# First feed-forward's up stage: the plain weight piece loaded on GpSimd's queue, the activations' accumulating store issued behind the weights' accumulates, 0.82 modulation dots a piece, and the second group of activations fetched one per piece

## The chip, the cores and the metric

The kernel runs on 1 core of one Trainium2 chip. Five engines work beside each other, each through its own instructions in order: TensorE (PE in the profile, with its weight loads as PEld), VectorE (DVE), ScalarE (ACT), GpSimd (POOL) and SyncE (SP). An instruction that waits holds up everything behind it on its engine. SP and POOL also issue DMAs here, so a DMA that has to wait for a buffer holds up the DMAs behind it in the same way. The metric is the device time of the whole program in microseconds (us); lower is better.

## The reference, cut to what matters

One layer: a half-step feed-forward on 256 latent tokens and 256 context tokens, a token mixing of attention and Hyena, and a second half-step feed-forward on the latent tokens alone. Each is normed and modulated by vectors that come out of `SiLU(c) @ w_ada`. All is float32. The change touches the first feed-forward's up projection and the start of its down projection.

```python
def swiglu(h, w_up, w_down):
    gate, up = jnp.split(h @ w_up, 2, axis=-1)
    return (jax.nn.silu(gate) * up) @ w_down

def half_ffn(s, m, slot, g, w_up, w_down):
    h = modulate(rms_norm(s, g), chunk(m, 3 * slot), chunk(m, 3 * slot + 1))
    return s + 0.5 * chunk(m, 3 * slot + 2) * swiglu(h, w_up, w_down)
...
        mod = (s_lat @ w_ada[l] + b_ada[l])[:, None, :]
        mod_c = (s_ctx @ w_ada[l] + b_ada[l])[:, None, :]
...
        x = half_ffn(x, mod, 0, g_norm[l, 0], w_ffn1_up[l], w_ffn1_down[l])
        ctx = half_ffn(ctx, mod_c, 0, g_norm[l, 0], w_ffn1_up[l], w_ffn1_down[l])
```

with `D_MODEL = 2048` and `D_FF = 5632`.

## The kernel before

**Precision.** Each float32 operand is split into a rounded high part and the remainder (`hi`, `lo`), and a product is three matmuls: hi times hi, hi times lo, lo times hi (`mm3`, L247 to L249). Casts to `hi` are ACT's work. The remainder is a subtraction on DVE, except in two places of this stage, where ACT writes minus `hi` and an accumulating DMA adds the original to it. Only POOL issues such accumulating DMAs here.

**The up stage.** The 5632 hidden columns are 44 columns `j` of 128, gate and up together. Columns 0 to 2 run beside the start of the program; columns 3 to 43 run one after the other in `Ffn.up(j)`, each in four pieces `kq` of 512 KB of weights. From column 9 on (`QUADS`), pieces 1 to 3 are each done with seven products in place of eight, and their weights go through `quad_weights`: ACT casts `bhi` (L436) and `whi` (L465), DVE makes `blo` (L439), three sums (L442 to L444) and `wlo` (L471). Their raw tiles come in by SP and rotate over four buffers.

Piece 0 is the **plain** one. Its weights for column j+1 are made in column j, after piece 1 (`prepare(j + 1, 0)`): a load into the tile `plain`, of which there is one buffer, two casts by ACT (L425), two negations by ACT (L426) and two accumulating DMAs that POOL issues (L427, `u<-plain`). The next load into `plain` has to wait until both accumulates have read it. In the kernel before, that load is issued by SP (`weight_load`, L224), in the same queue as the raw tiles and the tiles of the dots.

**The dots.** The modulation vectors of later stages are dot products that DVE makes between the matmul pieces: one dot takes a 512 KB tile `adaw` (two buffers, loaded by SP at L144) and multiplies and sums it with the row of `SiLU(c)` (L151). After each piece `ada_hook` adds a rate to a counter (`ADA_RATES[0]`) and asks for a dot when the counter passes one. The stage needs 128 of them, and columns 4 to 43 call the hook 160 times.

**The activations.** At the end of column j `close` or the sums behind it make the activation, and `keep` writes it to DRAM (`actd[j]`) as `hi` and remainder: two stores by POOL (L534, L535) and an accumulating DMA onto the second (L536), which has to wait until that store has landed.

**The down stage.** Groups of four activations are read back (`fetch`, L551, two DMAs of 256 KB each), two groups ahead of their use. The first two groups (`ORDERS[0]` begins 9, 8) are fetched in column 43: the first group after piece 0, the second after piece 1. Both are POOL's.

**What sets the order.** The program is written in one order and a scheduler places the instructions on each engine by their dependences; `then(x, ...)` and `issue_after` pin an instruction behind another one. POOL's DMAs share eight semaphores in turn, so one waits for the landing of the one eight before it.

Of the kernel before, what the change touches and what calls it, by code (L numbers as in the profile page):

```python
# [12 lines left out]
F32R = mybir.dt.float32r  # L13
AF = mybir.ActivationFunctionType
ALU = mybir.AluOpType
# [3 lines left out]
P = 128  # L19
# [4 lines left out]
JT = FF // P  # L24
GRP = 4
# [6 lines left out]
WAVE = 3  # L32
ADA_UP = (5, 7, 6, 8)
ADA_DOWN = (2, 3, 4)
ADA_RATES = (0.79, 1.15, 1.42)
QUADS = {3: 5, 2: 7, 1: 9}
GT = JT // GRP
PASSES = ((0, 1, 2, 3), (4, 5, 6, 7))
ORDERS = ((9, 8, 10, 7, 6, 5, 4, 3, 2, 1, 0), tuple(range(GT)))
# [23 lines left out]
def hybrid_layer_kernel(ctx: ExitStack, tc: tile.TileContext, a):  # L63
    nc = tc.nc
# [56 lines left out]
    done = [0]  # L121
# [100 lines left out]
    def weight_load(src, shape, queue=None, pool=None):  # L222
        raw = T(wp, shape, "raw", bufs=4) if pool is None else T(pool, shape, "plain", bufs=1)
        load = (queue or nc.sync).dma_start(raw, src)  # L224
        loads.append(load)
        if done[0]:
            last_load[0] = load
        return raw

# [37 lines left out]
    def then(behind, do, *args, **kw):  # L267

        with tc.issue_after(behind.ins):
            return do(*args, **kw)  # L270
# [89 lines left out]
    class Ffn:  # L360
        def __init__(self, wup, wdown, cm, hook=None):
            self.wup, self.wdown, self.cm = wup, wdown, cm
            self.hook = hook or (lambda: None)
            self.h = [None] * KT
            self.mm = mm3
            self.held = {}
            self.sums, self.first, self.begun = {}, {}, None
            self.wupq = a["w_up1q"]

        def open(self, alt=False):  # L370
# [47 lines left out]
        def prepare(self, j, kq):  # L418

            pool = adap if kq == 0 and j > WAVE else None  # L420
            raw = weight_load(self.wupq[j - WAVE, kq], (P, 2, 4, P), pool=pool)
            if kq == 0:
                hi, lo = ([U((P, 4, P), F32R) for _ in range(2)] for _ in range(2))
                for q in range(2):
                    S.copy(hi[q], raw[:, q])  # L425
                    S.activation(lo[q], hi[q].bitcast(F32), AF.Copy, scale=-1.0)  # L426
                    nc.gpsimd.dma_start(lo[q], raw[:, q].bitcast(F32R), accum_op=ALU.add)  # L427
                return [(hi, lo)]
            if not self.quads(j, kq):
                return [weight(None, (P, 2, 4, P), raw=raw)]  # L430
            return raw
# [58 lines left out]
        def up(self, j):  # L490
            todo = [list(self.products(j, kq)) for kq in range(4)]
            left = [sum(t[0] == bank for piece in todo for t in piece) for bank in range(4)]
            total = list(left)
            banks = [(PA, PB)[j % 2]((P, 2, L)) if n else None for n in left]
            for kq in range(4):
                w = self.ahead if kq == 0 else self.quad_weights(j, kq) if self.quads(j, kq) else self.prepare(j, kq)
                for bank, part, n, q, block, x in todo[kq]:
                    ps = banks[bank] if part is None else banks[bank][:, part, :]
                    xx = self.h[x] if part is None else self.sums[x[0]][x[1]]
                    left[bank] -= 1  # L500
                    mm3(ps, [t[q][:, block] if kq == 0 else t[:, q, block] for t in w[n]], xx, left[bank] == total[bank] - 1, left[bank] == 0)
                if j == JT - 1 and kq < 2:
                    for n in range(GRP):
                        self.fetch(ORDERS[0], kq, n)
                if j < JT - 1 and kq == 1:
                    self.ahead = self.prepare(j + 1, 0)
                self.hook()
            for kq in QUADS:
                if QUADS[kq] == j + 1:
                    self.install(kq)  # L510
            if not total[2]:
                return self.close(j, banks)
            g, v, u = tmp((P, 2, L)), U((P, 2, L)), T(up, (P, L), "mt", bufs=3)
            S.copy(g[:, 0, :], banks[2][:, 0, :])
            V.tensor_add(u, g[:, 0, :], banks[2][:, 1, :])
            V.tensor_add(g[:, 1, :], u, banks[3][:, 0, :])
            V.tensor_add(v[:, 0, :], u, banks[3][:, 1, :])
            V.tensor_add(v[:, 1, :], g[:, 1, :], banks[3][:, 1, :])
            V.tensor_add(g, g, banks[0])
            V.tensor_add(v, v, banks[1])  # L520
            S.activation(g, g, AF.Silu)
            V.tensor_mul(v, v, g)
            self.keep(j, v)

        def keep(self, j, act):

            if j == JT - 1:
                for s_, t in enumerate(split(act, (P, 2, L))):
                    nc.gpsimd.dma_start(actd[j][:, s_], t)
                return  # L530
            hi, minus = U((P, 2, L), F32R), U((P, 2, L), F32R)
            S.copy(hi, act)
            S.activation(minus, hi.bitcast(F32), AF.Copy, scale=-1.0)
            nc.gpsimd.dma_start(actd[j][:, 0], hi)  # L534
            nc.gpsimd.dma_start(actd[j][:, 1], minus)  # L535
            nc.gpsimd.dma_start(actd[j][:, 1], act.bitcast(F32R), accum_op=ALU.add)  # L536

        def fetch(self, order, n, jj):

# [36 lines left out]
        def down(self, after):  # L576

            uses = [(p, g) for p in range(len(PASSES)) for g in ORDERS[p]]
            for n, (p, g) in enumerate(uses):
                if g == ORDERS[p][0]:  # L580
                    banks = {2 * dq + i2: (PA, PB)[k // 2]((P, 2, L)) for k, dq in enumerate(PASSES[p]) for i2 in range(2)}
                order = [q for _, q in uses]
                if g == ORDERS[p][5]:
                    for dq in PASSES[p]:
                        for i in range(2):
                            xs[i][dq] = U((P, 2, L))
                            nc.sync.dma_start(xs[i][dq], a["xT"][i, dq])
                at = n - len(uses) + APART
                if at == 0:
                    break  # L590
                for jj, dq in enumerate(PASSES[p]):
                    self.fetch(order, n + 2, jj)
                    self.hook(p)
                    self.step(g, dq, banks, g == ORDERS[p][0], g == ORDERS[p][-1] or at == -1)
            yield
            rest = [g for _, g in uses[-APART:]]
            for part in (1, 0):
                banks = {dq: (PA if part else PB)((P, 2, L)) for dq in PASSES[-1]}
                for g in rest:
                    for dq in PASSES[-1]:  # L600
                        self.step(g, dq, banks, g == rest[0], g == rest[-1], part, None if part else after)
                if part:
                    yield
# [1067 lines left out]
```

## Time and profile before

| | us |
|---|---|
| median of 3 runs | 2658.39 (2653.15 to 2658.84) |
| the profiled execution | 2656.8 |
| its span, first to last instruction | 2655.0 |
| PE busy | 2606.0 |
| DVE busy | 1892.0 |
| ACT busy | 1114.4 |
| POOL busy | 253.8 |

In the profile a row of the timeline or of a group has the line of the program, the engine, the operation and the tiles as out<-in; `SPq` and `POOLq` are the instructions that issue DMAs. A row of the waits says which instruction waited for which, the us in total, how often, and the longest. A row of the stages has the stretch, its length, the busy time of each engine with its instructions, the clock that TensorE was granted, and the DMA share and rate. The up stage of columns 3 to 43 runs from 154.8 to 1038.4 us.

### The profile page before, as it was taken

The numbers are of one execution on the slowest core, as the hardware profiler recorded it, in microseconds if no ns is written. First come the engines' busy times: TensorE is split into PE (matmuls) and PEld (weight loads), VectorE is DVE, ScalarE is ACT, GpSimd is POOL, SyncE is SP. The second block draws the span as 40 slices with busy tenths as digits, with TensorE's granted clock in tenths as the row PEclk, the third lists the DMA queues.
The fourth block names the chain that finished last, engine by engine and source line by source line (L and its number), as shares of the span: only waits on it lengthen the run. The fifth ranks groups of instructions, "written<-read, shape, count | busy, mean of one in ns | idle before, by whom it ended". The sixth has DMA issues, their size and how long they took to land.

```text
span 2655.0 us, 38017 instructions
## 1 busy us (share of the span) xinstructions
PE 2606.0 (98%) x14480; PEld 2238.3 (84%) x14480; DVE 1892.0 (71%) x3051; ACT 1114.4 (42%) x1543; POOL 253.8 (10%) x395
## 2 busy tenths in 40 slices
PE   8999999999999998999999999999999999999999
PEld 5678989989899897888888988888788888888887
DVE  6767788878788877777989796889665555554444
ACT  5344444444444443112211455456554444444333
POOL 1121111111111112320011000000000000000000
PEclk9999999999999998999999999999999999999999
DMA  9978778878788788996798555345555666566664
GB/s 371 360 221 254 222 214 266 242 225 242 222 243 239 232 248 285 395 385 202 258 326 288 177 175 191 122 131 162 173 183 190 191 190 189 188 188 207 203 200 157
DMA packets 193923, 607.67 MB, mean 229 GB/s; under 512 B 22315, under 2 KB 25356, under 8 KB 189388
## 3 DMA queue, kind: packets, MB, share of 16 engines
q1 hardware_dynamic: 140444, 504.40, 57.1%
q0 software_dynamic: 53104, 100.72, 15.6%
q8 instruction: 113, 1.85, 0.3%
q14 instruction: 70, 0.57, 0.1%
q10 hardware_dynamic: 192, 0.13, 0.0%
HBM read 545.10 MB, written 38.57 MB: 220 GB/s over the span
## 4 chain that ended last, share of the span: by engine, by line
PE 78%; issue 9%; DMA 5%; DVE 4%; ACT 2%; POOL 1%; SPq 0%; POOLq 0%; DVEq 0%; ACTq 0%
PE pa L1331 10%; PE pa L1332 10%; PE pa L1330 10%; PE pa L247 6%; PE pa L248 6%; PE pa L249 6%; PE pb L247 6%; PE pb L249 6%; PE pb L248 6%; PE pa L255 3%; DMA act<-u 2%; PE pa L257 2%; PE pa L1044 1%; PE pa L1045 1%; DMA adaw<-in_w_adaT_dram 1%
## 5 line engine op out<-in xcount | busy, mean ns | idle before, releaser
L240 DVE TENSOR_TENSOR wlo<-raw,whi 128x1024 fp32r<-128x1024 f32 x487 | 595.1, 1223 | 473.3 <-ACT whi L236 471.9
L236 ACT CAST whi<-raw 128x1024 fp32r<-128x1024 f32 x487 | 512.4, 1053 | 881.4 <-PE pa L1332 413.4
L1330 PE MATMUL pa<-whi,u 128*128 128x512 f32 x1060 | 413.9, 391 | 0.0
L1331 PE MATMUL pa<-wlo,u 128*128 128x512 f32 x1060 | 412.8, 390 | 0.2 <-DVE wlo L240 0.2
L1332 PE MATMUL pa<-whi,u 128*128 128x512 f32 x1060 | 412.9, 390 | 0.0
L247 PE MATMUL pa<-u,whi 128*128 128x256 f32 (+1 forms) x928 | 314.4, 340 | 7.5 <-ACT whi L465 3.8
L249 PE MATMUL pa<-u,wlo 128*128 128x256 f32 (+1 forms) x928 | 312.1, 337 | 4.2 <-DVE wlo L471 4.2
L248 PE MATMUL pa<-u,whi 128*128 128x256 f32 (+1 forms) x928 | 312.2, 337 | 3.6 <-DMA u<-act 3.1
L249 PE MATMUL pb<-u,wlo 128*128 128x256 f32 (+1 forms) x920 | 305.1, 332 | 7.4 <-DVE wlo L471 7.3
L247 PE MATMUL pb<-u,whi 128*128 128x256 f32 (+1 forms) x920 | 306.6, 334 | 4.6 <-ACT whi L465 4.5
L248 PE MATMUL pb<-u,whi 128*128 128x256 f32 (+1 forms) x920 | 304.5, 331 | 0.0
L1332 PEld LDWEIGHTS pa<-whi,u 128*128 128x128 f32 x1060 | 198.9, 188 | 41.5
L1331 PEld LDWEIGHTS pa<-wlo,u 128*128 128x128 f32 x1060 | 199.0, 188 | 41.4 <-DVE wlo L240 0.6
L1330 PEld LDWEIGHTS pa<-whi,u 128*128 128x128 f32 x1060 | 199.0, 188 | 40.7
L151 DVE CUSTOM_DVE_ANT_0 adas<-adaw,crow,cond 128x1024 bf16<-128x1024 f32 x160 | 204.8, 1280 | 32.2 <-DMA adaw<-in_w_adaT_dram 30.3
L151 DVE CUSTOM_DVE_ANT_0 adas<-adaw,crow,mod 128x1024 bf16<-128x1024 f32 x160 | 204.9, 1281 | 31.1 <-DMA adaw<-in_w_adaT_dram 29.0
L247 PEld LDWEIGHTS pa<-u,whi 128*128 128x128 f32 x928 | 178.2, 192 | 31.9 <-issue 4.9
L249 PEld LDWEIGHTS pa<-u,wlo 128*128 128x128 f32 x928 | 178.7, 193 | 23.2 <-DVE wlo L471 5.7
L249 PEld LDWEIGHTS pb<-u,wlo 128*128 128x128 f32 x920 | 176.4, 192 | 25.0 <-DVE wlo L471 9.1
L248 PEld LDWEIGHTS pa<-u,whi 128*128 128x128 f32 x928 | 178.6, 193 | 21.6 <-DMA u<-act 4.0
L247 PEld LDWEIGHTS pb<-u,whi 128*128 128x128 f32 x920 | 176.5, 192 | 23.0 <-ACT whi L465 5.6
L248 PEld LDWEIGHTS pb<-u,whi 128*128 128x128 f32 x920 | 176.6, 192 | 15.7 <-issue 0.4
(356 smaller groups left out, 4643.8 us busy)
## 6 DMA issues: line engine op xcount, KB each, us to landing
adaw<-in_w_adaT_dram SPq DMA_DIRECT2D x224, 512.0 KB, 5.8
raw<-in_w_dn_dram SPq DMA_DIRECT2D x184, 512.0 KB, 4.1
raw<-in_w_up_dram SPq DMA_DIRECT2D x176, 512.0 KB, 3.5
raw<-in_w_up1q_dram SPq DMA_DIRECT2D x124, 512.0 KB, 5.0
u<-act POOLq DMA_DIRECT2D x136, 256.0 KB, 11.3
act<-u POOLq DMA_DIRECT2D x131, 256.0 KB, 4.9
wrow<-in_w_ada_dram SPq DMA_DIRECT2D x32, 1024.0 KB, 9.9
plain<-in_w_up1q_dram SPq DMA_DIRECT2D x40, 512.0 KB, 3.6
```

The source lines that it names most:

```text
L151: V.tensor_tensor_reduce(out=sc, in0=t, in1=crow[i][:, b * (D // 2) : (b + 1) * (D // 2)], scale=1.0, scalar=mcol if b else bada[:, c * KT ...
L236: S.copy(hi, raw)
L240: last_lo[0] = V.tensor_sub(lo, raw, hi.bitcast(F32))
L247: PE.matmul(ps, w[0], xx[0], start=start, stop=False)
L248: PE.matmul(ps, w[0], xx[1], start=False, stop=False)
L249: return PE.matmul(ps, w[1], xx[0], start=False, stop=stop)
L255: PE.matmul(ps, w[0], x, start=start, stop=stop)
L257: PE.matmul(ps[:, 0, :], w[1], x[:, 0, :], start=False, stop=False)
L1044: PE.matmul(p_, hh, wlo[:, k2, :], start=False, stop=False)
L1330: PE.matmul(ps[t], hi, w[0], start=start, stop=False)
L1331: PE.matmul(ps[t], hi, w[1], start=False, stop=False)
L1332: last = PE.matmul(ps[t], lo, w[0], start=False, stop=stop)
```

## The change

There are four edits. The load of `plain` is issued by POOL (`nc.gpsimd`), and no longer counts as the last weight load behind which SP places the next dot's load. The accumulating DMA of `keep` is kept back in `self.unadded` and issued by `add_act` after piece 1 of the next column, behind the second of the plain accumulates (`self.added`); for the first three columns it is issued at once. The rate of the dots goes from 0.79 to 0.82. In column 43 the second group's activations are fetched one after each of the pieces 1 to 3, and the fourth at the first step of the down stage.

```diff
-ADA_RATES = (0.79, 1.15, 1.42)
+ADA_RATES = (0.82, 1.15, 1.42)
...
-        if done[0]:
+        if done[0] and queue is None:
             last_load[0] = load
...
-            raw = weight_load(self.wupq[j - WAVE, kq], (P, 2, 4, P), pool=pool)
+            raw = weight_load(self.wupq[j - WAVE, kq], (P, 2, 4, P), nc.gpsimd if pool else None, pool)
...
-                    nc.gpsimd.dma_start(lo[q], raw[:, q].bitcast(F32R), accum_op=ALU.add)
+                    self.added = nc.gpsimd.dma_start(lo[q], raw[:, q].bitcast(F32R), accum_op=ALU.add)
...
-                if j == JT - 1 and kq < 2:
-                    for n in range(GRP):
-                        self.fetch(ORDERS[0], kq, n)
-                if j < JT - 1 and kq == 1:
-                    self.ahead = self.prepare(j + 1, 0)
+                if j == JT - 1:
+                    for n in range(GRP) if kq == 0 else (kq - 1,):
+                        self.fetch(ORDERS[0], min(kq, 1), n)
+                if kq == 1:
+                    if j < JT - 1:
+                        self.ahead = self.prepare(j + 1, 0)
+                    self.add_act()
                 self.hook()
...
-            nc.gpsimd.dma_start(actd[j][:, 1], act.bitcast(F32R), accum_op=ALU.add)
+            self.unadded = j, act
+            if j < WAVE:
+                self.add_act()
+
+        def add_act(self):
+            if self.unadded:
+                j, act = self.unadded
+                self.unadded = None
+                then(self.added, nc.gpsimd.dma_start, actd[j][:, 1], act.bitcast(F32R), accum_op=ALU.add)
...
                 for jj, dq in enumerate(PASSES[p]):
+                    if (n, jj) == (0, 0):
+                        self.fetch(order, 1, GRP - 1)
                     self.fetch(order, n + 2, jj)
```

The first place is POOL's queue in the middle of the up stage, where column 9's activation (`act_37`) is stored and the plain piece for column 11 (`plain_3123`) is finished. Before:

```order
L534 DMA act_37_117<-u_3031 128x512
L535 DMA act_37_117<-u_3032 128x512
L427 DMA u_3127<-plain_3123 128x512
L536 DMA act_37_117<-u_3020 128x512
L427 DMA u_3128<-plain_3123 128x512
L534 DMA act_38_118<-u_3269 128x512
```

The same queue one column later in the changed kernel, from the plain load for column 12 (`plain_3362`) to the one for column 13. The accumulate onto the activation has the line of `then`, L270:

```order
L224 DMA plain_3362<-in_w_up1q_dram 128x1024
L536 DMA act_38_118<-u_3271 128x512
L537 DMA act_38_118<-u_3272 128x512
L427 DMA u_3366<-plain_3362 128x512
L427 DMA u_3367<-plain_3362 128x512
L270 DMA act_38_118<-u_3260 128x512
L224 DMA plain_3602<-in_w_up1q_dram 128x1024
```

The accumulate onto the activation no longer stands between the two accumulates of the plain piece but behind both, and the next plain load stands behind it.

The second place is SP's queue at the same time, around the first raw tile of column 12 after its plain piece (`raw_3375` before, `raw_3379` now). Before:

```order
L144 DMA adaw_3194<-in_w_adaT_dram 128x1024
L224 DMA raw_3375<-in_w_up1q_dram 128x1024
L224 DMA plain_3361<-in_w_up1q_dram 128x1024
L144 DMA adaw_3253<-in_w_adaT_dram 128x1024
L224 DMA raw_3434<-in_w_up1q_dram 128x1024
L144 DMA adaw_3373<-in_w_adaT_dram 128x1024
L144 DMA adaw_3430<-in_w_adaT_dram 128x1024
```

And in the changed kernel:

```order
L144 DMA adaw_3198<-in_w_adaT_dram 128x1024
L224 DMA raw_3379<-in_w_up1q_dram 128x1024
L144 DMA adaw_3305<-in_w_adaT_dram 128x1024
L224 DMA raw_3438<-in_w_up1q_dram 128x1024
L144 DMA adaw_3375<-in_w_adaT_dram 128x1024
L224 DMA raw_3547<-in_w_up1q_dram 128x1024
L144 DMA adaw_3434<-in_w_adaT_dram 128x1024
```

The plain load is gone from SP's queue, and dot loads and raw tiles follow each other there.

The third place is POOL's queue in column 43, from the store of column 42's activation (`act_70`) to the fetches of the down stage's first group (`act_64` to `act_67`) and second group (`act_60` to `act_63`). Before:

```order
L534 DMA act_70_150<-u_10870 128x512
L551 DMA u_10905<-act_64_144 128x512
L535 DMA act_70_150<-u_10871 128x512
L551 DMA u_10906<-act_64_144 128x512
L551 DMA u_10909<-act_65_145 128x512
L551 DMA u_10910<-act_65_145 128x512
L536 DMA act_70_150<-u_10859 128x512
L551 DMA u_10913<-act_66_146 128x512
L551 DMA u_10914<-act_66_146 128x512
L551 DMA u_10917<-act_67_147 128x512
L551 DMA u_10918<-act_67_147 128x512
L551 DMA u_10980<-act_60_140 128x512
```

And in the changed kernel, where the fetch has line 561:

```order
L537 DMA act_70_150<-u_10891 128x512
L561 DMA u_10924<-act_64_144 128x512
L561 DMA u_10925<-act_64_144 128x512
L561 DMA u_10928<-act_65_145 128x512
L561 DMA u_10929<-act_65_145 128x512
L561 DMA u_10932<-act_66_146 128x512
L561 DMA u_10933<-act_66_146 128x512
L561 DMA u_10936<-act_67_147 128x512
L561 DMA u_10937<-act_67_147 128x512
L561 DMA u_10997<-act_60_140 128x512
L561 DMA u_10998<-act_60_140 128x512
L270 DMA act_70_150<-u_10879 128x512
```

The eight fetches of the first group now follow each other, the accumulate onto column 42's activation stands behind them and behind the first fetch of the second group.

More of the change, by code (lines that the diff above doesn't have):

```diff
@@ L366, in __init__ @@
             self.held = {}
-            self.sums, self.first, self.begun = {}, {}, None
+            self.sums, self.first, self.begun, self.unadded = {}, {}, None, None
             self.wupq = a["w_up1q"]
```

## The prediction

> **What bounds the kernel now.** I start with the busy shares of the page.
>
> ```profile
> span 2655.0 us, 38017 instructions
> PE 2606.0 (98%) x14480; PEld 2238.3 (84%) x14480; DVE 1892.0 (71%) x3051; ACT 1114.4 (42%) x1543; POOL 253.8 (10%) x395
> ```
>
> TensorE is the bound, and the change leaves its matmuls alone. So it can only win back time in which TensorE waits or runs at a lowered clock. The next view is what TensorE waited for over the whole program.
>
> ```profile
> PE pb L249 <- DVE wlo L471: 7.3, 7, 1.8
> PE pb L247 <- ACT whi L465: 4.5, 4, 1.9
> PE pa L249 <- DVE wlo L471: 4.2, 5, 1.3
> PE pa L247 <- ACT whi L465: 3.8, 2, 1.9
> PE pa L248 <- DMA u<-act: 3.1, 2, 2.0
> PE pa L247 <- DMA u<-act: 1.7, 2, 0.9
> ```
>
> The first four rows are weights that came late in the up stage, 7.3 + 4.5 + 4.2 + 3.8 = 19.8 us. The last two are activations that came late at the start of the down stage, 4.8 us. To price the first kind I take the pace of the columns. These are the first matmuls of columns 9 and 43, and then eight columns and the start of the down stage as stages.
>
> ```profile
> 284.78 0.40 PE L247 MATMUL pb<-u,u 128*128 128x512 f32 x1
> ...
> 1017.82 0.40 PE L247 MATMUL pb<-u,u 128*128 128x512 f32 x1
> ```
>
> ```profile
> 325.94:352.15 26.21, 22.84 (x153) 21.28 (x151) 18.13 (x29) 9.67 (x15) 3.75 (x5) 0.93 0.76 212
> ...
> 434.47:455.05 20.58, 20.58 (x153) 19.62 (x151) 17.16 (x31) 9.89 (x15) 3.77 (x5) 1.00 0.91 264
> 579.26:606.98 27.72, 23.12 (x153) 21.35 (x152) 18.59 (x33) 9.68 (x15) 3.76 (x5) 0.94 0.70 202
> 710.22:736.91 26.69, 23.37 (x152) 21.38 (x151) 17.35 (x29) 9.65 (x15) 3.77 (x5) 0.94 0.75 210
> 757.50:779.09 21.59, 20.83 (x153) 19.67 (x151) 18.19 (x29) 9.68 (x15) 3.76 (x5) 1.00 0.84 236
> 861.53:888.13 26.60, 22.82 (x152) 21.25 (x151) 18.30 (x32) 9.66 (x15) 3.77 (x5) 0.94 0.74 220
> 991.03:1017.81 26.78, 22.82 (x152) 21.25 (x151) 18.35 (x31) 9.67 (x15) 3.77 (x5) 0.94 0.74 225
> ...
> 1042.60:1053.00 10.40, 7.73 (x17) 5.27 (x18) 5.64 (x12) 0.00 (x0) 1.58 (x3) 0.51 1.14 405
> ```
>
> A column without a wait takes 20.58 us, all of it TensorE's. From 284.78 to 1017.82 there are 34 columns with the same matmuls, 733.0 us in place of 34 x 20.58 = 699.7: **33.3 us too long**. The five columns of 26 to 28 us hold 134.0 - 5 x 20.58 = 31.1 us of it, the rest is 2.2. In those five the granted clock is 0.93 or 0.94 too, some 1.7 us a column beside the waits themselves.
>
> Now one of the five, from late matmul back to its cause. The rows are SP's queue, DVE, POOL's queue, ACT, and SP's waits between 200 and 1017 us.
>
> ```profile
> 317.24 0.33 SPq L224 DMA_DIRECT2D raw<-in_w_up1q_dram  x1
> 323.85 0.33 SPq L224 DMA_DIRECT2D plain<-in_w_up1q_dram  x1
> 324.27 0.38 SPq L144 DMA_DIRECT2D adaw<-in_w_adaT_dram  x1
> ```
>
> ```profile
> 329.65 1.28 DVE L151 CUSTOM_DVE_ANT_0 adas<-adaw,crow,mod 128x1024 bf16<-128x1024 f32 x1 [4.61 <-DMA adaw<-in_w_adaT_dram]
> ...
> 333.40 1.22 DVE L471 TENSOR_TENSOR wlo<-raw,whi 128x1024 fp32r<-128x1024 f32 x1
> ```
>
> ```profile
> 311.70 0.55 POOL L534 DMA_DIRECT2D act<-u  x1 [14.29 <-ACT u L532]
> ...
> 313.54 0.88 POOL L427 DMA_DIRECT2D u<-plain  x1 [0.62 <-ACT u L426]
> 317.86 0.88 POOL L536 DMA_DIRECT2D act<-u  x1 [3.44 <-DVE raw L442]
> 318.40 1.24 POOL L427 DMA_DIRECT2D u<-plain  x1
> ```
>
> ```profile
> 311.97 0.60 ACT L425 CAST u<-plain 128x512 fp32r<-128x512 f32 x1
> ...
> 314.38 0.63 ACT L426 ACTIVATE u<-u 128x512 fp32r<-128x512 f32 x1
> ```
>
> ```profile
> SPq L224 <- DMA u<-plain: 277.5, 45, 9.4
> ```
>
> DVE stood 4.61 us before a dot whose tile SP issued only at 324.27, and `wlo` is in DVE's queue behind the dot. SP issued it late because the plain load stood ahead of it and waited for the second plain accumulate, which POOL issued at 318.40. That one was ready when ACT's negation ended, 314.38 + 0.63 = 315.0, but stood behind the activation's accumulate, which waited for its own store. So one queue's order is passed on through four engines. SP waited in this way 277.5 us in all; mostly it costs nothing, because the next dot's tile is not yet needed. It costs where dots fall close together:
>
> ```profile
> 325.94:352.15 26.21, 4.95 (x4) 0.93 0.76 212
> 372.73:393.31 20.58, 3.84 (x3) 1.00 0.89 265
> 434.47:455.05 20.58, 4.82 (x4) 1.00 0.91 264
> ```
>
> These count the dots of a column, four in the long one and three in a common one; the third row shows four without a loss. 0.79 x 4 is 3.16 a column, so a fourth falls about every sixth column, and the long ones lie six to twelve columns apart.
>
> **The change part by part.** The sum is made against the profiled execution's 2656.8 us (span 2655.0), which is 1.6 below the median of the runs.
>
> *Plain load on POOL, activation's accumulate behind both plain ones.* SP loses 40 issues and with them the wait above; the dot's tile of 324.27 had a free buffer since the dot before the last had ended, and is then held only by raw tiles. On POOL one DMA a column is added and one moved. Durations from issue to landing:
>
> ```profile
> adaw<-in_w_adaT_dram SPq DMA_DIRECT2D x224, 512.0 KB, 5.8
> ...
> plain<-in_w_up1q_dram SPq DMA_DIRECT2D x40, 512.0 KB, 3.6
> u<-plain POOLq DMA_DIRECT2D x80, 256.0 KB, 5.9
> ...
> raw<-in_w_up_dram POOLq DMA_DIRECT2D x9, 512.0 KB, 8.3
> ```
>
> Follow the column that begins at 305.36. The second accumulate moves from 318.40 to 315.0 and lands 5.9 later, at 320.9; the activation's accumulate keeps 317.9, since its store sets it. The plain load waits behind both and for the landing: issue at about 321, against 323.85 on SP. No trace shows this load on POOL. Its nearest rows are the same tile on SP, 3.6, and a tile of that size on POOL, 8.3; I take 8.3, which was measured in the crowded start. It then lands at 329.3. ACT reaches the next plain cast 311.97 - 305.36 = 6.6 us into a column, so at 325.94 + 6.6 = 332.5. That leaves 3.2 us to spare, and 7.9 with the shorter landing: at both ends the load costs nothing. What is queued behind the waiting load on POOL are the next activation's stores, not due before 332. The accumulates themselves land at 321 for a column that begins at 325.94. So I take out all 33.3 us.
>
> The Trainium skill (SBUF — State Buffer, section "SBUF: two separate sides") speaks against this edit: it says that GpSimd is kept from writing its DMA descriptors while VectorE runs an fp32 operation of a certain mode, and advises the other queues. The profile shows POOL's accumulates issued all through a stage where DVE is busy for 17 of 20.58 us, in 0.88 to 1.24 us each; by the example in that page's next section, 620 ns grown to 3100, the load would come 2.5 us later, an estimate inside the 3.2. No row here separates the two.
>
> *0.82 dots.* Over 160 pieces the counter now gives ten columns of four dots, and the 128th dot is asked for in the first piece of column 43. Work on DVE grows by 0.12 dots or 0.16 us a column, in some 3 us of idle. A column of four dots that no plain load blocked lost nothing (434.47) or 1.01 us (757.50); I take the middle, 0.5, so ten cost **5 us**, with 0 and 10 as ends. The 2.2 us of small losses are part of this.
>
> *The fetches of column 43.* POOL's queue there, and the landing that the down stage waited for:
>
> ```profile
> 1027.70 1.60 POOL L551 DMA_DIRECT2D u<-act  x3
> 1032.12 0.89 POOL L536 DMA_DIRECT2D act<-u  x1 [2.81 <-DMA act<-u]
> 1032.68 4.04 POOL L551 DMA_DIRECT2D u<-act  x7
> ```
>
> The first group's last four DMAs stood behind the activation's accumulate at 1032.12, and the second group's followed at once and shared the engines with them. Now the eight follow each other, the last four about 1032.68 - (1027.70 + 1.60) = 3.4 us earlier, with two DMAs behind them in place of eight. The late landings cost 4.8 us of waits, and the granted clock of 0.51 over 10.40 us, with PE busy for 7.73 of them, 7.73 x 0.49 = 3.8. I take out **8.6 us**. What comes earlier in exchange is the second row of `SiLU(c)`, 1 MB, with dot tiles for the next stage, since the last dot no longer holds their memory; they are due when column 43's last piece is under way, and most of the first group has landed by then. The fourth activation of the second group now stands behind the stores of column 43's own, but is not used before the second group's turn, some 20 us into the stage.
>
> Sum: 2656.8 - 33.3 + 5 - 8.6 = 2619.9. **Forecast 2620 us**, 1.4% faster.
>
> **Rivals.** *The start of the down stage still waits*, because the earlier 1 MB load and dot tiles take the place of the second group: 2620 + 8.6 = 2629. For it: the DMA share there is 1.14 already. Against: the first group is issued 3 to 4 us earlier.
>
> *Denser dots stall where plain no longer does.* Raw tiles still stand ahead of dot tiles on SP and wait for DVE. If three of the ten columns lose what the five lose now, 31.1 / 5 = 6.2 each, it is 2620 + 18.6 = 2639.
>
> *Slower, by the dots' own landing.* If a dot's tile takes too long from a free buffer to landing, whatever stands ahead of it, every column of four dots stalls, and the change makes ten of them: 2656.8 - 33.3 + 62 - 8.6 = 2677. It decides once the landing of 5.8 us outlasts the time between the dot that frees a buffer and the one that wants it, two dots later, in these columns one to two pieces of 20.58 / 4 = 5.1 us. Against it stands 434.47, four dots and no loss. The Trainium skill (DMA: Bandwidth & Descriptors, section "Issuing engines are not separate DMA queues") would have it near this: issuing from several engines saves only the issue time. Here the issue time includes SP's waits of up to 9.4 us, so the trace bears that out only in small part.
>
> *Slower, by the plain load.* POOL serves it late: once it lands more than 3.2 us after 329.3, ACT stands in every column before L425, with TensorE's casts behind it. Two us in each of 39 columns give 2620 + 78 = 2698. Against it: 8.3 is the slower of the two rows, and still leaves 3.2.
>
> **How the numbers follow.** Forecast 0.67; down stage still waits 0.12; dots stall in three columns 0.10; dots' own landing 0.06, of which 0.02 with so few stalls that nothing changes; plain load 0.05. Faster by over 0.2% (about what a measurement of this kernel can tell from no change) are the first three, 0.89; within it 0.02; slower 0.09. The range goes from 2611 (no dot costs, 2614.9, and 3 to 4 us for the spread of the runs) to 2641 (the third case and 2 us), and leaves out 0.11.
>
> **What would show it.** Right: no wait for `u<-plain` among SP's, no DVE wait for `adaw` over 2 us, 34 columns at 20.6 to 21.2 us, plain loads landing before 7 us into the next column, no wait for `u<-act` in PE's and a clock of 1.00 around 1010 us. Wrong: ACT idle before L425, columns of four dots at 26 us, or a clock of 0.5 at the start of the down stage.

## The result, and the profile after

| | kernel before | changed kernel |
|---|---|---|
| median of the runs, us | 2658.61 (2653.15 to 2661.36, 4 runs) | 2630.74 (2625.92 to 2638.44, 4 runs) |
| ratio, 95% interval | | 0.990 (0.9871 to 0.9929) |
| profiled execution, us | 2656.8 | 2625.9 |

The change makes the kernel 1.0% faster; 1.4% was forecast. The profiled execution of the changed kernel is the fastest of its four. The page of that execution:

```profile
span 2624.1 us, 38011 instructions
...
PE 2592.5 (99%) x14480; PEld 2228.7 (85%) x14480; DVE 1891.7 (72%) x3051; ACT 1115.3 (43%) x1543; POOL 275.2 (10%) x435
```

The work is the same to the instruction on TensorE. What TensorE waited for from 154.7 to 1060 us, by line (us in total, times, longest):

```profile
PE pb L249 <- DVE wlo L471: 3.1, 7, 0.8
PE pa L249 <- DVE wlo L471: 2.8, 5, 0.8
PE pa L249 <- DMA u<-plain: 2.1, 1, 2.1
```

The waits of 1.8 and 1.9 us for `whi` and `wlo` are gone, and those for `u<-act`. One for the plain weights is left, in column 4; the kernel before has one of 1.5 us there. The program as stages of the changed kernel: columns 3 to 8, columns 9 to 42, one column of four dots, the longest column of all, 40 us around the start of the down stage, and all from column 43 on. A row has the length, the busy time of PE, PEld, DVE, ACT and POOL, then the granted clock, the DMA share and the rate in GB/s.

```profile
154.71:286.91 132.20, 130.11 (x685) 112.40 (x684) 93.72 (x162) 59.23 (x94) 30.42 (x44) 0.99 0.85 244
...
286.91:997.19 710.28, 704.29 (x5102) 668.23 (x5101) 589.45 (x1001) 332.55 (x476) 145.52 (x203) 1.00 0.86 246
...
557.18:579.49 22.31, 21.21 (x152) 19.78 (x151) 17.48 (x30) 9.67 (x15) 4.32 (x6) 1.00 0.74 222
641.21:663.56 22.35, 21.33 (x152) 19.76 (x151) 17.02 (x28) 9.68 (x15) 4.32 (x6) 1.00 0.72 202
...
1000.00:1040.00 40.00, 40.00 (x237) 35.70 (x236) 25.81 (x40) 12.82 (x16) 15.22 (x28) 1.00 1.00 336
...
997.19:2624.10 1626.91, 1615.38 (x7726) 1353.20 (x7724) 1100.21 (x1632) 651.49 (x847) 75.19 (x141) 1.00 0.66 214
```

The kernel before has these two for the first and the last stretch:

```profile
154.76:284.78 130.02, 128.57 (x685) 111.22 (x684) 93.34 (x161) 58.95 (x94) 27.20 (x38) 1.00 0.83 239
...
1017.82:2655.00 1637.18, 1621.37 (x7726) 1356.35 (x7724) 1105.24 (x1645) 651.21 (x847) 74.98 (x141) 1.00 0.66 214
```

So columns 9 to 42 give 733.0 - 710.3 = 22.7 us, the rest of the program 10.3, and columns 3 to 8 take back 2.2: 2655.0 - 22.7 - 10.3 + 2.2 = 2624.2, the span of 2624.1. Against 34 x 20.58 = 699.7 there are still 10.6 us in columns 9 to 42, where the forecast left 5. Where they are, in the column at 557.18 (SP's queue, DVE, PE; and DVE's wait for dot tiles between 200 and 1017 us, 46.0 in 19 in the kernel before):

```profile
550.22 0.33 SPq L144 DMA_DIRECT2D adaw<-in_w_adaT_dram  x1
```

```profile
557.90 1.28 DVE L151 CUSTOM_DVE_ANT_0 adas<-adaw,crow,cond 128x1024 bf16<-128x1024 f32 x1 [1.61 <-DMA adaw<-in_w_adaT_dram]
```

```profile
571.12 0.38 PE L249 MATMUL pa<-u,wlo 128*128 128x256 f32 x1 [0.76 <-DVE wlo L471]
```

```profile
DVE adas L151 <- DMA adaw<-in_w_adaT_dram: 13.5, 13, 1.8
```

The dot still came 1.61 us late, though nothing for `plain` stands in SP's queue now. All that follows on DVE came later with it; ACT waited 1.11 us for DVE's L524, cast the next `whi` later in turn, and `wlo`, which needs that cast, is late a piece later. Column by column, eight columns hold 10.1 of the 10.6 us, and each of them has, within 1.5 us of its start, a dot that waited 0.6 to 1.8 us for its tile. The number of dots in a column does not decide it, as the dots of the longest column and of one that lost nothing show:

```profile
641.21:663.56 22.35, 3.84 (x3) 1.00 0.72 202
432.36:452.94 20.58, 5.12 (x4) 1.00 0.86 243
```

The median of the runs is 4.8 us above this execution; a second profile, below, shows where a slower one loses it.

### The profile page after: what moved, and what is told of

The parts are those of the page before. It is cut to its first block, busy times and chain, and to the rows that moved or that the text cites. A ratio compares the mean times of both kernels' runs of the same rounds, so it can differ in the third digit from the quotient of the medians.

```text
span 2624.1 us, 38011 instructions
## 1 busy us (share of the span) xinstructions
PE 2592.5 (99%) x14480; PEld 2228.7 (85%) x14480; DVE 1891.7 (72%) x3051; ACT 1115.3 (43%) x1543; POOL 275.2 (10%) x435
## 4 chain that ended last, share of the span: by engine, by line
PE 84%; DVE 6%; DMA 5%; ACT 3%; issue 2%; POOL 0%; SPq 0%; DVEq 0%; ACTq 0%; POOLq 0%
PE pa L1343 10%; PE pa L1342 10%; PE pa L1344 10%; PE pb L247 7%; PE pb L249 7%; PE pb L248 7%; PE pa L247 7%; PE pa L249 7%; PE pa L248 7%; PE pa L255 3%; DMA adaw<-in_w_adaT_dram 2%; PE pa L257 2%; DVE wlo L471 1%; PE pa L1056 1%; PE pa L1057 1%
```

## The experiments

All times are medians, the ratios against the kernel before on the same chip (2658.31, 2660.46 and 2659.59 us in the three groups of four kernels each).

### Each part alone: the plain load, the accumulate, the fetch, the rate

The kernel before with the load of `plain` on POOL and nothing else:

```diff
-        if done[0]:
+        if done[0] and queue is None:
...
-            raw = weight_load(self.wupq[j - WAVE, kq], (P, 2, 4, P), pool=pool)
+            raw = weight_load(self.wupq[j - WAVE, kq], (P, 2, 4, P), nc.gpsimd if pool else None, pool)
```

> The kernel before with one edit: the plain load is issued by POOL. The activation's accumulate still stands between the two plain accumulates, the rate is 0.79, the fetches are as before. Theory SP (a waiting plain load holds up the dots' tiles behind it on SP): the five long columns go, the 34 columns from 9 to 42 take 702 to 708 us in place of 733, the start of the down stage keeps its waits, about 2658 - 27 = 2631 us. Rival POOL (the accumulate between the two plain ones is what makes the load late): the load is just as late, the long columns stay or turn into ACT's waits before the plain casts, 2650 us or more.

2646.63 us, ratio 0.9956 (0.9941 to 0.9971).

The kernel before with the activation's accumulate behind both plain ones, and nothing else:

```diff
-                if j < JT - 1 and kq == 1:
-                    self.ahead = self.prepare(j + 1, 0)
+                if kq == 1:
+                    if j < JT - 1:
+                        self.ahead = self.prepare(j + 1, 0)
+                    self.add_act()
...
-            nc.gpsimd.dma_start(actd[j][:, 1], act.bitcast(F32R), accum_op=ALU.add)
+            self.unadded = j, act
+            if j < WAVE:
+                self.add_act()
```

> The kernel before with one edit: the activation's accumulate is issued behind both plain accumulates. Plain stays on SP, rate 0.79, fetches as before. Theory SP: the second plain accumulate lands about 3.4 us earlier, so each long column keeps what is left of DVE's wait of 4.6 to 6.2 us, 31 us of losses fall to about 12, some 2640 us. Rival POOL: all five long columns go, about 2629 us. In column 43 the accumulate now stands behind the first group's fetches, so a part of the 8.6 us at the start of the down stage may go as well; I expect half of it, 4 us, in both.

2641.75 us, ratio 0.9937 (0.992 to 0.9953). Columns 9 to 42 of the first kernel, and of the second, which keeps the load on SP, with SP's wait there:

```profile
291.82:1006.72 714.90, 706.25 (x5103) 668.04 (x5102) 583.43 (x990) 334.28 (x476) 146.40 (x203) 1.00 0.87 241
```

```profile
285.17:1003.68 718.51, 707.75 (x5103) 671.32 (x5102) 583.79 (x989) 332.48 (x476) 127.65 (x170) 1.00 0.85 239
```

```profile
SPq L224 <- DMA u<-plain: 178.8, 41, 8.4
```

Either edit alone takes out about half of the 33.3 us: 15.2 are left with the load moved, 18.8 with the accumulate moved. The second shortens SP's wait from 277.5 to 178.8 us without touching SP's queue, as the chain of the prediction has it. The first misses its expectation by 16 us, and falls between the two theories. TensorE's waits for the plain weights in it, from 291.8 to 1006.7 us; its other waits there, 4.5 us, are for `wlo`:

```profile
PE pa L249 <- DMA u<-plain: 2.0, 2, 1.4
PE pb L249 <- DMA u<-plain: 1.5, 1, 1.5
```

The second plain accumulate still stands behind the activation's, so the plain weights themselves now come late at times, and ACT waited for the plain load before L425 eight times, 9.1 us in all, as the rival in the expectation has it. Columns 3 to 8 took 135.2 us (130.0 before), and the start of the down stage waits as it did, 5.3 us for `u<-act`.

The two edits that remain, each alone:

```diff
-                if j == JT - 1 and kq < 2:
-                    for n in range(GRP):
-                        self.fetch(ORDERS[0], kq, n)
+                if j == JT - 1:
+                    for n in range(GRP) if kq == 0 else (kq - 1,):
+                        self.fetch(ORDERS[0], min(kq, 1), n)
...
+                    if (n, jj) == (0, 0):
+                        self.fetch(order, 1, GRP - 1)
```

> The kernel before with one edit: the second group's activations are fetched one per piece. The accumulate onto column 42's activation still stands between the fetches of the first group. If the pile of sixteen fetches makes the first group late: no wait for u<-act, no lowered clock at the start of the down stage, 2658 - 8.6 = 2650 us. If the accumulate in the middle makes it late: about half of the 4.8 us of waits stays, and with it the lowered clock, 2655 us. The up stage's five long columns stay in both.

2658.77 us, ratio 1.0002 (0.9993 to 1.0012).

```diff
-ADA_RATES = (0.79, 1.15, 1.42)
+ADA_RATES = (0.82, 1.15, 1.42)
```

> The kernel before with one edit: 0.82 dots a piece. Theory SP: ten columns of four dots in place of six, behind a plain load that still waits on SP, so 8 to 10 long columns at about 6 us in place of five, less 2 us at the end of the stage: 2658 + 16 to 30 = 2674 to 2688 us. Rival (the long columns come from something that falls every sixth column and not from the fourth dot): 2657 to 2660 us.

2659.13 us, ratio 1.0003 (0.9993 to 1.0012). The start of the down stage with the fetch edit alone, and columns 9 to 42 with the rate alone:

```profile
1042.00:1056.00 14.00, 10.42 (x34) 7.40 (x35) 7.85 (x14) 2.11 (x3) 1.06 (x2) 0.76 1.12 404
```

```profile
286.50:1027.84 741.34, 716.01 (x5102) 677.62 (x5101) 589.96 (x1001) 332.11 (x476) 128.19 (x170) 0.99 0.83 237
```

The fetch edit alone leaves the wait (5.7 us for `u<-act`, 4.8 before) and the lowered clock, and neither of its two expectations came: the eight fetches of the second group were not what delayed the first. The rate alone costs 8.3 us in the columns (741.3 against 733.0), far less than expected: six of its twelve columns of four dots are long, by 4.7 to 7.7 us, where the kernel before has five of nine. It gains at the start of the down stage, as shown below, and no change of the whole can be measured. The four parts sum to -11.7 - 16.6 + 0.5 + 0.8 = -27.0; the changed kernel has -27.9.

### The changed kernel again

> The changed kernel as it is, beside the kernel before in many more rounds, and as the kernel that the next three are read against. From its own 2630.7 us: 2627 to 2635, 0.99 of the kernel before. A second profile tells whether its 10.6 us over 34 x 20.58 in columns 9 to 42 and the late start of columns 3 to 8 (2.2 us over before) come back, or were of that one execution.

2631.56 us, ratio 0.9902 (0.9887 to 0.9917), as before. Its profiled execution was the slowest of the five, 2638.75 us. Columns 3 to 8, 9 to 42, and the rest:

```profile
155.66:292.71 137.05, 131.25 (x686) 113.27 (x684) 93.79 (x162) 59.47 (x94) 30.43 (x44) 0.98 0.83 235
...
292.71:1005.17 712.46, 705.51 (x5102) 668.49 (x5101) 589.07 (x1000) 333.03 (x476) 145.44 (x203) 1.00 0.86 245
...
1005.17:2637.00 1631.83, 1620.38 (x7726) 1357.25 (x7724) 1100.39 (x1633) 652.85 (x847) 75.11 (x141) 1.00 0.67 214
```

Beside the first profile of the changed kernel, 4.9 us more are in columns 3 to 8, 2.2 in columns 9 to 42, and 4.9 in the rest. The rest has a lowered clock far behind the change: 0.90 over the stretch from 1500 to 1550 us, where the first profile had 1.00 and the kernel before 0.97. The same wait of TensorE stands ahead of it in all three, 2.5 us for a `wlo`, and the 20 us behind that wait differ (the kernel before, the first and the second profile of the changed one):

```profile
1538.00:1558.00 20.00, 19.95 (x90) 16.63 (x91) 16.77 (x32) 10.03 (x19) 0.00 (x0) 0.92 0.59 171
```

```profile
1508.00:1528.00 20.00, 19.93 (x96) 16.67 (x97) 18.09 (x36) 11.38 (x21) 0.00 (x0) 1.00 0.62 186
```

```profile
1516.00:1536.00 20.00, 19.95 (x74) 16.67 (x75) 13.32 (x27) 8.27 (x16) 0.00 (x0) 0.74 0.52 158
```

So 0 to 5 us are won or lost there from one execution to the next, whatever the change does; on this point the first profile was lucky. Columns 3 to 8 are near the change, and are taken up below.

### What is left in columns 9 to 42: the rate, and the number of buffers

The changed kernel with the old rate:

```diff
-ADA_RATES = (0.82, 1.15, 1.42)
+ADA_RATES = (0.79, 1.15, 1.42)
```

> The changed kernel with the old rate 0.79, so six to seven columns of four dots in place of ten. Buffer theory (each column of four dots still costs about 1 us, because a tile can only be asked for when the dot two before it has ended): columns 9 to 42 lose some 4 us less than in the changed kernel, 6 to 7 in place of 10.6, and about 3 us come back as dots left over at the end of the stage, so the time is within 3 us of the changed kernel's. Rival, that the rate carries part of the gain by itself: 5 us or more slower than the changed kernel. Rival, that denser dots cost what the long columns of before did: 10 us or more faster.

2633.27 us, ratio 0.9901 (0.9887 to 0.9914). Columns 9 to 42:

```profile
290.03:995.75 705.72, 703.67 (x5103) 668.14 (x5101) 583.20 (x989) 333.59 (x476) 145.50 (x203) 1.00 0.85 243
```

6.0 us over 699.7, as the buffer theory has it. The rest took 1632.3, with 2.7 us of waits for `u<-act`, and the whole comes out the same: 0.82 moves lost time from the start of the down stage into the columns.

Then three buffers for the dots' tiles, paid for with two buffers `u`, and as a control the two `u` fewer alone:

```diff
-        return T(up, shape, "u", dt, 58)
+        return T(up, shape, "u", dt, 56)
...
-    adap, adaw_bufs = adap_cm.__enter__(), 2
+    adap, adaw_bufs = adap_cm.__enter__(), 3
```

> The changed kernel with three buffers for the dots' tiles in place of two; the 56 in place of 58 buffers u pay for the memory. Buffer theory: the rest of 10.6 us over 34 x 20.58 in columns 9 to 42 falls under 4, DVE's waits for adaw from 13.5 us in 13 to under 4, the longest under 1, and the kernel is 6 to 8 us faster than the changed one. Rival, that DVE is simply full in a column of four dots (17 us of work and its order): the excess stays at 9 to 11 us though the waits for adaw are gone, same time. Rival, that two u fewer make ACT or POOL wait: slower, with waits for u that were not there.

2633.45 us, ratio 0.9902 (0.9887 to 0.9917).

> The changed kernel with 56 in place of 58 buffers u and nothing else, to tell what the three-buffer run paid for its memory. Theory that the two buffers u were what it lost: a column 9 of about 25 us with DVE waiting for act<-u at L395, columns 9 to 42 at some 15 us over 34 x 20.58, 3 to 6 us slower than the changed kernel. Rival, that the third buffer does nothing for the time and the u are enough: same as the changed kernel.

2643.10 us, ratio 0.9938 (0.9925 to 0.995). Columns 9 to 42 and column 9 alone, then DVE's waits for DMAs from 284 to 1017 us; first with three buffers and 56 `u`, then with two buffers and 56 `u`:

```profile
293.19:1001.85 708.66, 703.98 (x5103) 669.18 (x5102) 590.86 (x1005) 336.59 (x477) 145.56 (x203) 1.00 0.87 246
293.19:318.64 25.45, 22.39 (x152) 21.03 (x151) 18.70 (x32) 9.95 (x15) 4.31 (x6) 0.93 0.78 221
```

```profile
DVE u L395 <- DMA act<-u: 2.3, 1, 2.3
```

```profile
292.81:1012.61 719.80, 709.31 (x5102) 671.28 (x5101) 591.04 (x1004) 334.13 (x477) 145.26 (x203) 1.00 0.85 243
292.81:319.46 26.65, 23.73 (x153) 22.27 (x151) 18.77 (x32) 9.92 (x15) 4.30 (x6) 0.87 0.78 224
```

```profile
DVE adas L151 <- DMA adaw<-in_w_adaT_dram: 12.9, 11, 2.6
DVE u L395 <- DMA act<-u: 2.8, 1, 2.8
```

With the third buffer DVE has no wait for `adaw` left. Without column 9 the excess is 708.7 - 25.5 - 33 x 20.58 = 4.1 us; with two buffers and the same `u` it is 719.8 - 26.7 - 679.1 = 14.0. So the third buffer is worth 9.7 us where the `u` are equal (2643.1 against 2633.5), and two `u` fewer cost 11.5 (2643.1 against 2631.6): 6.1 of it in column 9, where DVE waits for a buffer that an accumulate onto an activation still reads; where the rest lies the profiles don't settle. The two cancel, and the expected 6 to 8 us did not come. The rival, that DVE is simply full, falls: the same work on DVE took the shorter time.

### The fetches, in the changed kernel

The changed kernel with the second group fetched at once after piece 1:

```diff
-                if j == JT - 1:
-                    for n in range(GRP) if kq == 0 else (kq - 1,):
-                        self.fetch(ORDERS[0], min(kq, 1), n)
+                if j == JT - 1 and kq < 2:
+                    for n in range(GRP):
+                        self.fetch(ORDERS[0], kq, n)
...
-                    if (n, jj) == (0, 0):
-                        self.fetch(order, 1, GRP - 1)
```

> The changed kernel with the second group's eight fetches after piece 1 at once, as before; the other three edits stay. Theory that the accumulate in the middle of the first group's fetches was what made the down stage wait: same time within 1 us, since the accumulate now stands behind both groups, at most 2 to 3 us of waits for u<-act and no lowered clock at the start of the down stage. Rival, that the eight fetches at once take the first group's bandwidth: waits of 4 us and a clock of 0.5 as before, 5 to 8 us slower.

2629.83 us, ratio 0.9891 (0.9878 to 0.9905). Column 43 and the first 40 us of the down stage:

```profile
999.14:1060.00 60.86, 60.86 (x330) 52.98 (x329) 43.84 (x70) 17.89 (x21) 20.05 (x37) 1.00 1.00 339
```

TensorE is busy throughout, at a clock of 1.00, without the fetch edit. Together with the run of the fetch edit alone this settles that fetching one per piece adds nothing measurable. The accumulate that no longer stands among the first group's fetches is not the whole of the rest, though. The 60 us from column 43 on with the accumulate moved alone, the rate alone, and the changed kernel at the old rate:

```profile
1003.68:1063.68 60.00, 57.11 (x310) 48.97 (x309) 47.16 (x76) 16.79 (x20) 18.95 (x35) 1.00 1.01 347
```

```profile
1027.84:1087.84 60.00, 57.44 (x300) 49.28 (x299) 38.58 (x61) 16.60 (x20) 22.91 (x43) 0.94 1.03 344
```

```profile
995.75:1055.75 60.00, 57.29 (x304) 48.97 (x303) 45.99 (x75) 16.59 (x20) 18.69 (x35) 0.97 1.03 352
```

In each some 2.6 to 2.9 us of waits for `u<-act` are left. Counted over the first 300 matmuls from column 43 on, the kernel before took 63.97 us and the changed one 54.61; the accumulate alone took 58.38, the rate alone 60.60, the changed kernel at the old rate 59.75. So the accumulate's place brings 5.6 of the 9.4 us by itself, the rate 3.4, and only both together bring all. How the rate does it, no run tells; with it fewer dots are left over behind the columns.

### Column 4

A column 4 without waits takes 21.76 us. It took 23.55 in the kernel before, and 25.73 and 30.57 in the two profiles of the changed one. SP's queue, POOL's queue and PE in the slower of the two (the third fence is the row of the DMA view between 160 and 190 us, its last number the median us from issue to landing, as in the rows of that kind further on):

```profile
168.88 5.77 SPq L224 DMA_DIRECT2D raw<-in_w_up1q_dram  x2
175.52 0.33 SPq L144 DMA_DIRECT2D adaw<-in_w_adaT_dram  x1
```

```profile
175.40 0.88 POOL L270 DMA_DIRECT2D act<-u  x1 [6.98 <-DMA act<-u]
175.95 2.14 POOL L427 DMA_DIRECT2D u<-plain  x2
...
183.86 0.80 PE L249 MATMUL pa<-u,u 128*128 128x512 f32 x1 [5.80 <-DMA u<-plain]
```

```profile
u<-plain POOLq DMA_DIRECT2D x2, 256.0 KB, 8.9
```

In the first profile that median is 7.8 us. In the kernel before, SP's waits from 155 to 185 us and the same landing:

```profile
SPq L224 <- DMA u<-plain: 37.1, 2, 21.0
```

```profile
u<-plain POOLq DMA_DIRECT2D x2, 256.0 KB, 5.3
```

The accumulates of the first three columns still stand ahead of the plain ones and wait for their stores, in both kernels. But before, SP stood still for 21.0 us at the plain load for column 5, and nothing of its own was under way when the plain accumulates were issued; now it loads raw and dot tiles there. The other profiles agree: column 4 takes 25.7 to 30.6 us in all seven profiles with the plain load on POOL and these accumulates in place, and 22.4 to 23.6 in the four with the load on SP. Two runs take this apart. First, the first columns' accumulates held back like the others:

```diff
-            self.unadded = j, act
-            if j < WAVE:
-                self.add_act()
+            self.unadded.append((j, act))
...
-            if self.unadded:
-                j, act = self.unadded
-                self.unadded = None
+            for j, act in self.unadded:
...
+            self.unadded = []
```

> The changed kernel with the accumulates onto the activations of columns 0 to 2 held back too and issued behind both plain accumulates of column 4, as for every later column. Theory that they stand ahead of these on POOL's queue and wait for their stores: the wait for u<-plain in column 4 (5.8 us in the last profile of the changed kernel, 2.1 in the first) goes, with the lowered clock at 182 us; columns 3 to 8 take 128 us in place of 132 to 137; 5 to 7 us faster than the changed kernel, 2624 to 2627. Rival, that the plain weights of column 4 come late because of other transfers, whatever stands ahead: column 4 stays at 25 us or more, same time.

2627.21 us, ratio 0.9882 (0.9869 to 0.9896). Then one load back on SP:

```diff
-            raw = weight_load(self.wupq[j - WAVE, kq], (P, 2, 4, P), nc.gpsimd if pool else None, pool)
+            raw = weight_load(self.wupq[j - WAVE, kq], (P, 2, 4, P), nc.gpsimd if pool and j != WAVE + 2 else None, pool)
```

> The changed kernel with one load put back: the plain piece of column 5 is loaded by SP again, all others by POOL. In the kernel before, SP stood at this load from 159.7 to 180.8 us and issued nothing. Theory that this wait kept raw tiles and dots' tiles off the DMA engines while the plain accumulates of column 4 were under way: they land within 5 us of their issue again (7.9 in the changed kernel), column 4 takes 23 to 24 us in place of 25.7 to 30.6, and the time is 2 to 6 us below the changed kernel's. Rival, that the accumulates are slow because of the stores and accumulates on POOL's own queue around them: no change.

2624.77 us, ratio 0.987 (0.9856 to 0.9883). The plain accumulates on POOL and column 4 as a stage in the first of these runs, then SP's wait (155 to 185 us), the landing and column 4 in the second:

```profile
163.88 0.88 POOL L427 DMA_DIRECT2D u<-plain  x1 [0.65 <-ACT u L426]
165.05 0.87 POOL L427 DMA_DIRECT2D u<-plain  x1 [0.29 <-ACT u L426]
```

```profile
176.90:198.66 21.76, 21.76 (x97) 18.02 (x96) 15.24 (x25) 10.20 (x17) 4.86 (x7) 1.00 0.96 273
```

```profile
SPq L224 <- DMA u<-plain: 20.7, 1, 20.7
```

```profile
u<-plain POOLq DMA_DIRECT2D x2, 256.0 KB, 5.5
```

```profile
177.93:201.30 23.37, 22.06 (x98) 17.95 (x96) 14.71 (x25) 10.08 (x17) 4.42 (x7) 1.00 0.96 252
```

Both theories hold. Issued 12 us earlier, the plain accumulates may take as long as they like; issued late as ever, but with SP standing still, they land in 5.5 us and not in 8.9. One load put back on the queue that the change cleared makes the kernel faster than the changed one, with intervals of the ratio that just don't meet (0.9883 and 0.9887). The interval of the changed kernel's first four runs is wider and does meet it, but eight of its nine executions took longer than the longest of these four. The other run shows its gain in the profile, but its interval overlaps that of the changed kernel.

### Both together

The accumulates held back, with three buffers for the dots' tiles and 56 `u` (the edits of above):

> The changed kernel with both: the first columns' accumulates held back, and three buffers for the dots' tiles with 56 u. If both theories hold and add up: columns 3 to 8 at 128 us, the dots' waits gone, the long column 9 perhaps still there: 2621 to 2624. If the held activations run the u short with only 56, a wait for act<-u in columns 3 to 9 takes it back: 2626 to 2632.

2624.16 us, ratio 0.9872 (0.9857 to 0.9887). Columns 3 to 8 took 128.3 us, columns 9 to 42 took 708.7 with a column 9 of 26.5. This and the run with one load back on SP are the fastest measured; both beat the kernel before by 35 us and the changed one by some 7. Three buffers without the loss of the `u` would need 4 KB a partition more, and was not tried.

## Why the prediction was right, and where it was off

- **What bounds, and the chain** were right. The long columns came from POOL's order, passed on through SP's plain load to the dots' tiles: either link taken out alone removes about half of the excess, and both together all five long columns.
- **33.3 us out** held as to the long columns. The chance that denser dots stall for 6.2 us each, or that the plain load comes late in every column, did not come true: in the first profile the longest column from 9 on takes 22.35 us. The load on POOL landed in 6.3 us at the median, between the ends of 3.6 and 8.3, and ACT stood before L425 for 0.2 us in all there.
- **+5 for the dots** was too small: 10.6 and 12.7 us in two profiles. The step priced columns of four dots, and put those of two and three at nothing. By the dots that start in a column, the ten of four lost 6.7 and 5.0 us, near the price; the others lost 3.9 and 7.7. (The kernel before has nine columns of four dots already, not one in six.) The runs show a limit that the step had only as a rival: two buffers, so that a tile is asked for when the dot two before it has ended. At 550.22 to 557.90 that was 7.7 us, and a third buffer ends these waits. In this form it costs 0.5 to 2.4 us in a column, not the 6.2 of that rival.
- **"At both ends the load costs nothing"** failed in one place. It was worked out on the column at 305.36, and in column 4 the plain accumulates are late already. Moving the load off SP freed SP there, and its transfers lengthened theirs: 2.2 us lost in columns 3 to 8 in the first profile, 7.0 in the second (137.05 against 130.02). None of the rivals had it. With the dots' term it makes up the distance to the median.
- **8.6 us at the start of the down stage** came out in size, 9.4 by the first 300 matmuls; the rest of the program took 10.3 less. The account of it was right in one half only: the accumulate's place brings 5.6, the fetch per piece, which I counted in, brings nothing, and the rate, which I had not counted there, brings the rest.
- **The sum** against the first profile: 2619.9 + 5.6 (dots) + 2.2 (columns 3 to 8) - 1.7 (rest, 8.6 - 10.3) = 2626.0, measured 2625.9. Against the second: 2619.9 + 7.7 + 7.0 + 3.2 (rest, 8.6 - 5.4) + 0.9 (a later start of column 3) = 2638.7, measured 2638.75. These sums close because their terms are read off the stages of the same profiles; they say where the distance lies, and prove no cause. The terms of the rest hold the clock behind 1500 us, which differs from one execution to the next by no doing of the change. The median of 2630.7 lies between.
- **Moving the load to another queue** was worth 11.7 us alone, because what SP lost was waiting in order. The Trainium skill ("DMA: Bandwidth & Descriptors", section "Issuing engines are not separate DMA queues") says that another issuing engine saves only issue time, and does not cover this. The same section says that DMAs run on the same DMA engines whichever engine issues them; column 4 agrees (5.3 against 8.9 us).
- **The plain load on POOL** was issued in 0.55 us beside a busy DVE. The Trainium skill ("SBUF — State Buffer", section "SBUF: two separate sides") says that GpSimd cannot write DMA descriptors during certain operations of VectorE; whether the landing, 6.3 us against 3.6 on SP, is longer by that or by the company on the engines, no run tells apart.

## What to carry to other kernels

Where an instruction that waits stands in a queue of transfers, follow who is held up behind it before pricing the wait: here a wait on POOL cost time on TensorE by way of SP and DVE, and its cure was a place in a queue, not less work. Then ask what the held queue will issue once it is free and what it will share the DMA engines with; a wait that seems pure loss may be keeping traffic off a transfer that is late already. When an edit is made of parts, run each alone and the whole without it: two of four parts here carried nearly all, the rate gave in one place what it took in another, and the fetches did nothing measurable.

## What the runs showed of the hardware

- Two accumulating DMAs of 256 KB, issued together, took a median of 5.3 to 5.5 us from issue to landing while SP issued nothing, and 8.9 with raw and dot tiles issued in the 7 us ahead of them (7.8 in the first profile).
- In column 4 a single wait of TensorE of 2.1 us went with a lowered clock (first profile: 25.73 us, of which 21.76 are work, 2.1 the wait, and the rest a granted clock of 0.93), and one of 1.45 us did not (23.55 us at 1.00). With a wait of 5.8 us the column lost 3.0 more to the clock. Each is one execution.
- The length of a wait alone did not decide it: behind one and the same wait of 2.5 us near 1510 to 1540 us, the granted clock over 20 us was 1.00, 0.92 and 0.74 in three executions.
